# Second feed-forward matrix of an encoder block: Strassen's seven products for eight in three quarters of it, weight sums added in place by DMAs

## The chip, the core and the metric

The kernel runs on one core of a Trainium2 chip. The core has five engines, each with its own instruction queue that is worked through in order: PE (TensorE, matrix products into PSUM, eight banks of 128 x 512 float32), ACT (ScalarE), DVE (VectorE), POOL (GpSimd) and SP (SyncE). They meet only through semaphores. Sixteen DMA engines move data between HBM and SBUF; transfers are issued from the queues of SP, ACT and POOL. The metric is the device time of one execution in microseconds.

## The reference

One encoder block in float32 on 256 tokens of width 2048. What matters here is its last part, the feed-forward part:

```python
h = _layernorm(DEEPNORM_ALPHA * h + mix, ln1_g[l], ln1_b[l])
ff = jnp.square(jax.nn.relu(h @ w_ff1[l])) @ w_ff2[l]
h = _layernorm(DEEPNORM_ALPHA * h + ff, ln2_g[l], ln2_b[l])
```

`w_ff1` is 2048 x 8192, `w_ff2` is 8192 x 2048. Before it stand a gated linear attention branch, a Hyena branch (short convolution, long convolutions by transforms), their gates and an output projection, none of which the change touches in what it computes.

## The kernel before

**Precision.** Every float32 matrix product is made of three products of a narrower format: a value is split into a high part (a cast, on ACT) and a low part (value less high part, on DVE), in `split_hi_lo` (L84 to L86), and hi x hi, hi x lo and lo x hi are summed in PSUM. Weights come from HBM unsplit, so every weight passes through ACT and DVE once.

**Weights.** All weights lie in `wblk`, an array of blocks of 128 x 2048, in the order in which they are used. `fetch` (L95) takes the next block: a DMA on SP into one of three `raw` buffers, then two splits of 128 x 1024 into the `whi` and `wlo` buffers (three each). `next_block` fetches one more and gives the oldest. `resident` loads the last blocks of a stage into their own tiles.

**First feed-forward matrix.** `ff1(qi)` makes one quarter (2048 columns) of the hidden activations, channels on the partitions: for each of 16 blocks of 128 channels `channel_products` runs 16 products of 128 x 512 (both parts of the activation at once, L146) and 16 of 128 x 256 (L150). `channel_sum` adds the two halves of the PSUM bank (ACT L158, DVE L159). Each pair of blocks is squared behind a relu (DVE L1078) and split into the tile `f` that the second matrix reads.

**Second feed-forward matrix.** `ff2(qi)` adds one quarter's share to the residual: four groups of 512 output columns, each with four weight blocks. `token_products` goes through a block's four pieces of 128 x 512 (128 hidden channels by 512 output columns), and for both blocks of 128 tokens runs three products (L205 to L207): 24 products of 128 x 512 a weight block. `add_ff` adds the PSUM sum to `z1`, the residual (L1092 in the first quarter, where it also scales the residual, L1094 later).

**Order.** The quarters run as `ff1(0), ff1(1), ff2(0), ff1(2), ff2(1), ff1(3), ff2(2), ff2(3)`. The scheduler of the framework orders each engine's queue by program order, priorities and a timeline of its own. The last column group of the last quarter uses weights that were made resident, and the final layer norm is worked into it.

**PSUM and SBUF.** Four PSUM banks are `mm` (`psum_main`) and four `sd` (`psum_side`). The tile `zr` has four rows of 2048: two are `z1`, two hold the scale and shift rows of a layer norm.

**Adding DMAs.** The short convolution (`short_conv`) has DMAs that add: `nc.gpsimd.dma_start(dst, src, accum_op=ALU.add)` on L742 adds SBUF rows shifted by one partition to a tile in SBUF. Its large ones have 127 partitions of 4 KB.

Of the kernel before, what the change touches and what calls it, by code (L numbers as in the profile page):

```python
# [9 lines left out]
F32 = mybir.dt.float32  # L10
F32R = mybir.dt.float32r
# [16 lines left out]
CW = D // NCH  # L28
QT = 4
W_OUT_END = 177  # L30
OPENING = 5
PIECES = tuple((k, 1) for k in range(6)) + tuple((k, 2) for k in range(6, KT, 2))

# [9 lines left out]
def block_kernel(  # L43
# [40 lines left out]
    def split_hi_lo(hi, lo, src):  # L84
        return (nc.scalar.copy(hi, src),  # L85
                nc.vector.tensor_tensor(lo, src, hi.bitcast(F32), op=ALU.subtract))  # L86
# [44 lines left out]
    def next_block():  # L131
        fetch()
        return queue.popleft()
# [3 lines left out]
    def channel_psum(name):  # L137
        return psum_main(name).rearrange("p (a b) -> p a b", a=2)
# [19 lines left out]
            nc.scalar.activation(low, ps[:, 1], AF.Copy, scale=scale)  # L158
            nc.vector.scalar_tensor_tensor(dst, ps[:, 0], scale, low, op0=ALU.mult, op1=ALU.add)  # L159

    def channel_pair(act, name, dst=None, scale=1.0, begun=None):
        if dst is None:
            dst = base.tile([P, 2, L], F32, tag="sum", name=f"{name}_s")
        for c in range(2):
            if begun:
                ps, parts, n = begun.pop(0)
                finish_block(ps, act, parts, n)
            else:
                ps = channel_psum(f"{name}_{c}")
                parts = next_block()  # L170
                for h in range(2):
                    channel_products(ps, act, parts[h], range(8 * h, 8 * h + 8))
            channel_sum(dst[:, c], ps, f"{name}_l{c}", scale)
            pump()
        return dst

    def high_by_tokens(ps, act, half, kts, ts):
        for kt in kts:
# [55 lines left out]
    def act_tile(pool, tag, name):  # L234
        return pool.tile([P, KT, 2, L], F32R, tag=tag, name=name)
# [679 lines left out]

    tc.keep_in_program_order(nc.scalar.preload_act_table_set("natural_log_exp_and_others"))

    def resident(slots):
        parts = []
        for hi, lo in slots:  # L920
# [4 lines left out]
            for h in range(2):  # L925
                cs = slice(h * 1024, (h + 1) * 1024)
                split_hi_lo(hi[:, cs], lo[:, cs], raw[:, cs])
            parts.append([(hi[:, 0:1024], lo[:, 0:1024]), (hi[:, 1024:], lo[:, 1024:])])
        return parts

    def halves(pool, tag, name):
        t = pool.tile([P, 4, D], F32R, tag=tag, name=name)
# [39 lines left out]
    rows1 = load_rows(0)  # L972
    turn_b, turn_i = dfth, dftl
    for i, t in ((0, turn_b), (1, turn_i)):
        raw = ep.tile([P, 4, P], F32, tag="aff", bufs=1, name=f"turn{i}")
# [19 lines left out]
    stop_at[0] = nblk  # L995
    hT = act_tile(ep, "hT", "hT")
    lows = []
    for tb in range(NT):
# [34 lines left out]
            turn(at, n)  # L1033


    fts = {}

    def begin_three():
        blocks = [queue.popleft(), [], []]
        hx, lx = (ep.tile([P, D], F32R, tag=t, name=f"{t}_f") for t in ("xh", "xl"))  # L1040
# [29 lines left out]
        fetch()  # L1070
        return begun

    def ff1(qi):
        begun = begin_three() if qi == 0 else []
        f = act_tile(ep, "f", f"f{qi}") if qi % 2 == 0 else act_tile(base, "xT", f"f{qi}")
        for c2 in range(8):
            r = channel_pair(hT, f"f{qi}_{c2}", begun=begun)
            sq = nc.vector.scalar_tensor_tensor(r, r, 0.0, r, op0=ALU.max, op1=ALU.mult)  # L1078
            s = slice(2 * c2, 2 * c2 + 2)
            split_hi_lo(f[:, s, 0], f[:, s, 1], r)  # L1080
            if qi == 0 and 2 <= c2 < 6:
# [3 lines left out]
        fts[qi] = f  # L1085

    st2 = ep.tile([P, NT, 8, 6], F32, tag="bst", bufs=2, name="bst2")

    def add_ff(ps, tb, at, n, qi, last=False):
        zc = z1[:, tb, at:at + n]  # L1090
        if qi == 0:
            nc.vector.scalar_tensor_tensor(zc, zc, ALPHA, ps, op0=ALU.mult, op1=ALU.add)  # L1092
        else:
            nc.vector.tensor_tensor(zc, zc, ps, op=ALU.add)  # L1094
        if qi == QT - 1:
            for i in range(n // 256):
                nc.vector.bn_stats(st2[:, tb, at // 256 + i, :], zc[:, i * 256:(i + 1) * 256])
            if not last:
                nc.vector.tensor_tensor(zc, zc, rows2[:, 0, at:at + n], op=ALU.mult)

    def ff2(qi, groups=4):
        for g in range(groups):
            pss = token_group(fts[qi], f"w2_{qi}{g}")
            for tb in range(NT):
                add_ff(pss[tb], tb, g * 512, 512, qi)

    ff1(0)
    rows2 = load_rows(2)
    ff1(1)
    ff2(0)  # L1110
    ff1(2)
    ff2(1)
    ff1(3)
    ff2(2)
    stop_at[0] = nblk - 4
    ff2(3, 3)
    parts = resident(halves(ep, "f", "wr2") + halves(ep, "hT", "wr3"))
    minus = ep.tile([P, P], F32, tag="minus", name="minus")
    nc.vector.tensor_scalar(minus, ident, -1.0, None, op0=ALU.mult)
    unit = ep.tile([P, P], F32R, tag="unit", name="unit")  # L1120
    nc.scalar.copy(unit, ident)
    zg = tuple(ep.tile([P, D], F32R, tag=t, name=f"{t}_z") for t in ("xh", "xl"))
    for at in (0, 768):
        split_hi_lo(zg[0][:, at:at + 768], zg[1][:, at:at + 768], z1[:, 1, at:at + 768])

    def affine(tb, at, n, rs, nb):
        zc = z1[:, tb, at:at + n]
        t = ep.tile([P, 512], F32, tag="aff", bufs=1, name=f"aff{tb}_{at}")[:, 0:n]
# [7 lines left out]
    token_products([ps], fts[3], parts, [0], 0)  # L1136
    pss = [psum_main(f"w2_33_1{ch}") for ch in range(2)]
    add_ff(ps, 0, 1536, 512, 3)
# [4 lines left out]
    column_products([None, pss], fts[3], parts, [1], 0)  # L1143
    CENTRED = ((0, 512), (512, 512), (1024, 256), (1280, 256))
    po = {}
    for at, n in CENTRED[:3]:
        po[at] = psum_side(f"lo{at}")
        for part in zg:
            tc.keep_in_program_order(MM(po[at], unit, part[:, at:at + 512], start=(part is zg[0]), stop=False))
    po[1280] = po[1024][:, 256:]  # L1150
    add_ff(pss[0][:, 0:256], 1, 1536, 256, 3, last=True)
    late = z1[:, 1, 1536:2048]
    with tc.high_priority(), tc.issue_after(done.ins):
        add_ff(pss[1][:, 0:256], 1, 1792, 256, 3, last=True)
# [12 lines left out]
        nc.vector.tensor_tensor(rs, y, t, op=ALU.mult)  # L1167
# [8 lines left out]
def _layout(a):  # L1176
# [24 lines left out]
    for i in range(NCH // 2):  # L1201
# [1 line left out]
    f1 = chan(a["w_ff1"][0])  # L1203
    w2 = a["w_ff2"][0]
    f1q = [f1[16 * i:16 * (i + 1)] for i in range(QT)]
    f2q = [tok(w2[D * i:D * (i + 1)]) for i in range(QT)]
    g1, g2 = tok(seg["g"][:, :D]), tok(seg["g"][:, D:])
    wblk = np.concatenate(
        [chan(ga), chan(seg["q"]), chan(seg["k"]), tok(seg["r"]), tok(seg["v"]), g1]
        + ubl + [g2, tok(a["w_hy_o"][0]), tok(a["w_out"][0])]  # L1210
        + [f1q[0], f1q[1], f2q[0], f1q[2], f2q[1], f1q[3], f2q[2], f2q[3]], axis=0)
# [100 lines left out]
```

## Time and profile before

| | |
|---|---|
| median of three runs | 1826.89 us (1826.2 to 1827.17) |
| profiled execution, its own time and its span | 1826.2 us |
| matrix products on TensorE | 8931 |
| weight blocks loaded (`raw<-wblk`, 1024 KB each) | 300 |
| median time from issue to landing of such a load | 4.9 us |

Engines in the profile are PE, PEld (weight loads of TensorE, which run beside its products), DVE, ACT, POOL and SP. In the DMA rows q1 is the queue that SP issues to, q0 the one of POOL and q10 the one of ACT. A row of a group of instructions gives line, engine, operation, tiles, shapes and count, then the busy time and the mean duration in ns, then the idle time of the engine ahead of them and who ended it. A row of waits gives who waited for whom, the sum, the number and the longest. In a stretch of the trace the columns are the busy time (and count) of PE, PEld, DVE, ACT and POOL, the granted clock, the DMA share and GB/s. A row of the POOL line gives shortest, median and longest duration in ns.

### The profile page before, as it was taken

Reading aid. Unit: us, or ns where it says so; the run is one execution under the profiler, and the core shown is the slowest. Engines: PE = TensorE matmul, PEld = TensorE weight load, DVE = VectorE, ACT = ScalarE, POOL = GpSimd, SP = SyncE. Lnnn points to the kernel's source line nnn. Section 1 sums busy time; section 2 is a strip of 40 time slices with the busy share of each in tenths; the row PEclk is TensorE's granted clock in tenths of the full one; section 3 lists DMA queues with packets and bytes.
Section 4 is the critical chain, followed back from the end, with each engine's and each line's share of the span. In section 5 each row is a group of like instructions: output and inputs, shape, how many; then the busy total and the mean of one; then the engine's idle time right before and its main releaser. Section 6 shows DMA issues by size and latency. Waiting matters only on the chain.

```text
span 1826.2 us, 22887 instructions
## 1 busy us (share of the span) xinstructions
PE 1817.0 (99%) x8931; PEld 1533.8 (84%) x8931; DVE 1286.8 (70%) x1587; ACT 924.1 (51%) x1207; POOL 80.4 (4%) x121
## 2 busy tenths in 40 slices
PE   9999999999999999999999999999999999999998
PEld 7888888888888888888888889888888888888887
DVE  6789887875689899898755567666545655565467
ACT  6678668865444444444544445444434443443332
POOL 1011110000111101020000000000000000000000
PEclk9999999999999999999999999999999999999999
DMA  8668765345788979796544763545554555555453
GB/s 326 222 257 293 253 220 204 141 162 210 235 281 255 320 249 274 259 281 230 215 186 185 288 252 137 210 185 188 193 196 186 193 195 187 195 195 187 188 197 123
DMA packets 65452, 399.55 MB, mean 219 GB/s; under 512 B 8280, under 2 KB 10856, under 8 KB 24640
## 3 DMA queue, kind: packets, MB, share of 16 engines
q1 hardware_dynamic: 47808, 336.61, 49.1%
q0 software_dynamic: 10480, 41.81, 9.9%
q10 hardware_dynamic: 7056, 19.67, 3.0%
q8 instruction: 70, 1.15, 0.2%
q14 instruction: 38, 0.31, 0.0%
HBM read 369.28 MB, written 16.25 MB: 211 GB/s over the span
## 4 chain that ended last, share of the span: by engine, by line
PE 97%; DMA 1%; DVE 1%; ACT 0%; issue 0%; SPq 0%; DVEq 0%; POOL 0%; ACTq 0%
PE f L146 12%; PE f L150 6%; PE w L205 6%; PE w L207 6%; PE w L206 6%; PE g L206 3%; PE g L205 3%; PE g L207 3%; PE ux L207 3%; PE ux L206 3%; PE ux L205 3%; PE k L146 2%; PE v L206 2%; PE v L205 2%; PE v L207 2%; PE go L206 2%
## 5 line engine op out<-in xcount | busy, mean ns | idle before, releaser
L86 DVE TENSOR_TENSOR wlo<-raw,whi 128x1024 fp32r<-128x1024 f32 x584 | 712.3, 1222 | 356.5 <-ACT whi L85 353.4
L85 ACT CAST whi<-raw 128x1024 fp32r<-128x1024 f32 x584 | 614.0, 1053 | 576.1 <-PE w L207 186.5
L146 PE MATMUL f<-hT,whi 128*128 128x512 f32 x984 | 235.1, 391 | 0.0
L146 PEld LDWEIGHTS f<-hT,whi 128*128 128x128 f32 x984 | 180.8, 188 | 35.0
L206 PE MATMUL w<-wlo,f 128*128 128x512 f32 x480 | 186.7, 389 | 0.0
L207 PE MATMUL w<-whi,f 128*128 128x512 f32 x480 | 186.7, 389 | 0.0
L205 PE MATMUL w<-whi,f 128*128 128x512 f32 x480 | 167.4, 389 | 0.0
L150 PEld LDWEIGHTS f<-hT,wlo 128*128 128x128 f32 x984 | 126.2, 191 | 4.8
L150 PE MATMUL f<-hT,wlo 128*128 128x256 f32 x984 | 127.7, 283 | 0.0
L158 ACT ACTIVATE f_l<-f 128x256 f32<-128x256 f32 x64 | 24.6, 384 | 162.2 <-PE f L146 159.3
L207 PEld LDWEIGHTS w<-whi,f 128*128 128x128 f32 x480 | 90.1, 188 | 18.8
L205 PEld LDWEIGHTS w<-whi,f 128*128 128x128 f32 x480 | 90.1, 188 | 18.7
L206 PEld LDWEIGHTS w<-wlo,f 128*128 128x128 f32 x480 | 90.1, 188 | 18.7
L159 DVE SCALAR_TENSOR_TENSOR f_s<-f,f_l 128x256 f32<-128x256 f32 x64 | 27.2, 425 | 105.0 <-ACT f_l L158 105.0
L206 PE MATMUL g<-wlo,xT 128*128 128x512 f32 x256 | 100.1, 391 | 0.0
L207 PE MATMUL ux<-whi,xT 128*128 128x512 f32 x256 | 99.9, 390 | 0.0
L207 PE MATMUL g<-whi,xT 128*128 128x512 f32 x256 | 99.8, 390 | 0.0
L206 PE MATMUL ux<-wlo,xT 128*128 128x512 f32 x256 | 99.6, 389 | 0.0
L205 PE MATMUL g<-whi,xT 128*128 128x512 f32 x256 | 93.8, 392 | 0.0
L205 PE MATMUL ux<-whi,xT 128*128 128x512 f32 x256 | 89.7, 389 | 0.0
L206 PEld LDWEIGHTS g<-wlo,xT 128*128 128x128 f32 x256 | 48.1, 188 | 10.1 <-DVE wlo L86 0.2
L206 PEld LDWEIGHTS ux<-wlo,xT 128*128 128x128 f32 x256 | 48.1, 188 | 10.1
(428 smaller groups left out, 3235.4 us busy)
## 6 DMA issues: line engine op xcount, KB each, us to landing
raw<-wblk SPq DMA_DIRECT2D x300, 1024.0 KB, 4.9
Td<-T POOLq DMA_DIRECT2D x32, 384.0 KB, 5.5
conv_sb<-conv_rows SPq DMA_DIRECT2D x12, 1024.0 KB, 11.7
Tl<-Td POOLq DMA_DIRECT2D x16, 768.0 KB, 9.1
w<-w4s ACTq DMA_DIRECT2D x16, 512.0 KB, 5.7
xw<-first SPq DMA_DIRECT2D x5, 896.0 KB, 13.4
zr<-ln_rows ACTq DMA_DIRECT2D x4, 1024.0 KB, 10.5
cx<-shift POOLq DMA_DIRECT2D x8, 508.0 KB, 8.4
```

Of the source, the lines that this page charges most:

```text
L85: return (nc.scalar.copy(hi, src), nc.vector.tensor_tensor(lo, src, hi.bitcast(F32), op=ALU.subtract))
L86: nc.vector.tensor_tensor(lo, src, hi.bitcast(F32), op=ALU.subtract))
L146: MM(ps[:, :, ts], hi[:, js], act[:, kt, :, ts], start=(kt == 0 and opens), stop=(kt == KT - 1))
L150: MM(ps[:, 0, ts], lo[:, js], act[:, kt, 0, ts], start=False, stop=False)
L158: nc.scalar.activation(low, ps[:, 1], AF.Copy, scale=scale)
L159: nc.vector.scalar_tensor_tensor(dst, ps[:, 0], scale, low, op0=ALU.mult, op1=ALU.add)
L205: MM(pss[tb], sh, wh, start=(kt == 0), stop=False)
L206: MM(pss[tb], sh, wl, start=False, stop=False)
L207: MM(pss[tb], sl, wh, start=False, stop=(kt == KT - 1))
```

## The change

For three of the four quarters the second matrix is taken in blocks of 2 x 2: 256 hidden channels by 1024 output columns by 256 tokens, each halved in every direction. Eight block products become seven, by Winograd's form of Strassen's scheme. Four forms of the activations are sums and differences (`forms`: three subtractions on DVE), the other three are blocks themselves. The weight side needs sums of pieces of 128 x 512, and these are made by DMAs that add into the loaded tile.

One weight load (`ring_load`) holds 1536 of the four pieces' 2048 columns. There are 48 of them, called slots here, 8 for each of two column groups of each quarter. For slot `p`, in a ring of four tiles:

- `plain_split(p)` splits the three pieces as loaded (1536 columns). Then a DMA on POOL adds the fourth piece from HBM to two of the three (512 KB).
- `pair_split(p)` splits these two sums (1024 columns), and two DMAs on POOL follow: a piece from HBM is added to the first of them (256 KB), and that sum is added, from SBUF to SBUF, to the third (256 KB).
- `last_split(p)` splits these two (1024 columns). With that the seven weight forms have been made.

The products of a slot come in three parts: `plain` in slot `p`, the pair one slot later, the last two sums two slots later. Between them each slot runs one block of the first matrix for the next quarter, whose weights come in half blocks (`half_load`, `half_split`) through three buffers of their own. The seven sums of a column group stay in PSUM over eight slots, so seven banks are taken and one is left for the first matrix. `take_sum` brings them into `z1` and into `zacc`, which takes the two rows that held the layer norm's scale and shift, and `join_sums` puts them together at the end (16 operations of 512 columns). The last quarter keeps its eight products. The block order in `wblk` alternates between the matrices.

```diff
-    ff2(0)
-    ff1(2)
-    ff2(1)
-    ff1(3)
-    ff2(2)
-    stop_at[0] = nblk - 4
-    ff2(3, 3)
...
+    def plain_split(p):
+        raw, n = ring_tile(p), FF_PAIRS + 2 * p
+        hi = ep.tile([P, D], F32R, tag="xh", name=f"b_h{p}")[:, 0:1536]
+        lo = ep.tile([P, 1536], F32R, tag="wx", name=f"b_l{p}")
+        split_hi_lo(hi, lo, raw[:, 0:1536])
+        nc.gpsimd.dma_start(raw[:, 0:1024].rearrange("p (a b) -> p a b", a=2),
+                            wblk[n, :, None, 1536:2048].broadcast_to([P, 2, 512]), accum_op=ALU.add)
+        pieces_of[p, 0] = list(zip(units(hi), units(lo)))
+
+    def pair_split(p):
+        raw, n = ring_tile(p), FF_PAIRS + 2 * p
+        hi, lo = weight_half(n, 0)
+        split_hi_lo(hi, lo, raw[:, 0:1024])
+        nc.gpsimd.dma_start(raw[:, 0:512], wblk[n, :, 512:1024], accum_op=ALU.add)
+        nc.gpsimd.dma_start(raw[:, 1024:1536], raw[:, 0:512], accum_op=ALU.add)
+        pieces_of[p, 1] = list(zip(units(hi), units(lo)))
+
+    def last_split(p):
+        raw = ring_tile(p)[:, 0:1536].rearrange("p (u c) -> p u c", c=512)[:, 0:3:2]
+        fa_slot(4)
+        hi, lo = (t[:, 7168:8192] for t in fa)
+        split_hi_lo(*(t.rearrange("p (u c) -> p u c", c=512) for t in (hi, lo)), raw)
+        pieces_of[p, 2] = list(zip(units(hi), units(lo)))
...
+    def forms(i, plain=False):
+        q, slot = quads(i), fa_slot(i)
+        if plain:
+            split_hi_lo(slot[:, 0, 0:4], slot[:, 1, 0:4], q)
+            return
+        split_hi_lo(slot[:, 0, 0:3], slot[:, 1, 0:3], q[:, 1:4])
+        t = base.tile([P, 4, P], F32, tag="dftl", name=f"fw{i}")
+        TT = nc.vector.tensor_tensor
+        TT(t[:, 0:2], q[:, 0:1].broadcast_to([P, 2, P]), q[:, 1:3][:, ::-1], op=ALU.subtract)
+        TT(t[:, 2], q[:, 1], t[:, 0], op=ALU.subtract)
+        TT(t[:, 3], q[:, 3], t[:, 2], op=ALU.subtract)
+        split_hi_lo(slot[:, 0, 3:7], slot[:, 1, 3:7], t)
...
+    def form_products(pss, p, which, ks):
+        i = p % 8
+        slot = fa_slot(i)
+        for k, (wh, wl) in zip(ks, pieces_of.pop((p, which))):
+            ps, f = pss[k], FORM[k]
+            sh, sl = slot[:, 0, f], slot[:, 1, f]
+            MM(ps, sh, wh, start=(i == 0), stop=False)
+            MM(ps, sh, wl, start=False, stop=False)
+            MM(ps, sl, wh, start=False, stop=(i == 7))
+        if i == 7:
+            for k in ks:
+                take_sum(p // 16, p // 8 % 2, k, pss[k])
...
+    def half_split(j):
+        hi, lo = weight_half(FF_PAIRS + 1 + j // 2 * 2, j % 2)
+        split_hi_lo(hi, lo, half_at.pop(j))
+        half_parts[j] = (hi, lo)
+        if j + 3 < 2 * SLOTS:
+            half_at[j + 3] = half_load(j + 3)
...
+                at = 2 * c2 + c
+                if at == 12:
+                    for j in range(3):
+                        half_at[j] = half_load(j)
+            sq = squares(c2)
+            forms(c2)
+            if c2 == 5:
+                for j in range(3):
+                    half_at[j] = half_load(j)
...
+    def ff_pairs():
+        pss = [psum_side(f"w{j}") if j < 4 else psum_main(f"w{j}") for j in range(7)]
+        joins = []
+        for s in range(SLOTS + 2):
+            if s < SLOTS:
+                form_products(pss, s, 0, (0, 1, 2))
+                if s + 1 < SLOTS:
+                    plain_split(s + 1)
+            if 1 <= s <= SLOTS:
+                form_products(pss, s - 1, 1, (3, 4))
+            if s < SLOTS:
+                pair_split(s)
+            if 2 <= s:
+                form_products(pss, s - 2, 2, (5, 6))
+                if s == SLOTS - 7:
+                    joins = join_sums(0)
+            if s + 2 < SLOTS:
+                ring_load(s + 2)
+            if s >= 10 and (s - 10) % 16 < 8:
+                forms((s - 10) % 16, s >= 2 * 16 + 10)
+            if s < SLOTS:
+                ps = channel_psum(f"f{s // 16 + 1}_{s % 16}")
+                for h in range(2):
+                    channel_products(ps, hT, half_parts.pop(2 * s + h), range(8 * h, 8 * h + 8))
+                    if h == 0 and 1 <= s:
+                        last_split(s - 1)
+                    if s + 1 < SLOTS:
+                        half_split(2 * s + 2 + h)
+                i, c = divmod(s % 16, 2)
+                quad_sum(i, c, ps, f"f{s // 16 + 1}_l{s % 16}")
+                if c:
+                    squares(i)
```

The relu and the square of the hidden activations, one operation on DVE before, are two passes on ACT now (`squares`). Scratch tiles at the end of the kernel (`own`, `spare`, `zg`) are laid into other buffers.

More of the change, by code (lines that the diff above doesn't have):

```diff
@@ L916, in block_kernel, with resident_pieces @@
     tc.keep_in_program_order(nc.scalar.preload_act_table_set("natural_log_exp_and_others"))
-    def resident(slots):
-        parts = []
-        for hi, lo in slots:
+    def resident_pieces(parts):
+        for part in parts:
             n = fetched[0]
@@ L924, in resident @@
             nc.sync.dma_start(raw, wblk[n])
[L925 to L928, printed above, removed]
-        return parts
+            for h, (hi, lo) in enumerate(part):
+                split_hi_lo(hi, lo, raw[:, h * 1024:(h + 1) * 1024])
+        return parts
+    def resident(slots):
+        return resident_pieces([[(hi[:, c:c + 1024], lo[:, c:c + 1024]) for c in (0, 1024)] for hi, lo in slots])
     def halves(pool, tag, name):
@@ new lines, in block_kernel, with quads @@
+    first_quads = {}
+    def quads(i):
+        m = i % 5 if ring else 1 + i % 2
+        if m not in first_quads:
+            if m == 1:
+                first_quads[m] = base.tile([P, 4, P], F32, tag="dfth", name="fr1")
+            elif m == 2:
+                first_quads[m] = base.tile([P, 4, P], F32, tag="sum", name="fr2")
+            else:
+                spare = ring_tile((0, None, None, 1, 2)[m])[:, 1536:2048]
+                first_quads[m] = spare.rearrange("p (a b) -> p a b", b=P)
+        return first_quads[m]
@@ new lines, in block_kernel, with __getitem__, ring_load, units @@
+    class Quarter:
+        def __getitem__(self, at):
+            _, kt, part, ts = at
+            return fa_slot(kt // 2)[:, part, ((1, 0), (3, 2))[kt % 2][ts.start // P]]
+    SLOTS = 48
+    def ring_load(p):
+        nc.sync.dma_start(ring_tile(p)[:, 0:1536], wblk[FF_PAIRS + 2 * p, :, 0:1536])
+    pieces_of = {}
+    def units(t):
+        return [t[:, k * 512:(k + 1) * 512] for k in range(t.shape[1] // 512)]
+    def plain_split(p):
[6 more added lines that the diff above has]
+        pieces_of[p, 0] = list(zip(units(hi), units(lo)))
@@ L1087, in block_kernel, with add_ff @@
     st2 = ep.tile([P, NT, 8, 6], F32, tag="bst", bufs=2, name="bst2")
-    def add_ff(ps, tb, at, n, qi, last=False):
+    def add_ff(ps, tb, at, n, last=False):
         zc = z1[:, tb, at:at + n]
[L1091 to L1099, printed above, removed]
@@ new lines, in add_ff, with quarters @@
+        if not last:
+            nc.vector.tensor_tensor(zc, zc, rows2[:, 0, at:at + n], op=ALU.mult)
+    ff1_first()
+    for p in range(2):
+        ring_load(p)
+    plain_split(0)
+    for j in range(2):
+        half_split(j)
+    ff_pairs()
+    rows2 = load_rows(2)
+    f3 = Quarter()
+    for n in range(3):
+        fetch()
+    for g in range(3):
+        pss = token_group(f3, f"w2_3{g}")
+        for tb in range(NT):
+            add_ff(pss[tb], tb, g * 512, 512)
+    def quarters(*tiles):
+        at = [t[:, k:k + 1024] for t in tiles for k in range(0, t.shape[1], 1024)]
+        return [[(at[0], at[1]), (at[2], at[3])], [(at[4], at[5]), (at[6], at[7])]]
```

171 lines of the change are left out of this document (125 added, 46 removed).

## The prediction

> **What bounds the kernel now.** I read the page's first sections and its chain of waits, then the waits of the feed-forward part alone (1040 us to the end), then stretches of that part.
>
> ```profile
> span 1826.2 us, 22887 instructions
> ...
> PE 1817.0 (99%) x8931; PEld 1533.8 (84%) x8931; DVE 1286.8 (70%) x1587; ACT 924.1 (51%) x1207; POOL 80.4 (4%) x121
> ...
> PEclk9999999999999999999999999999999999999999
> DMA  8668765345788979796544763545554555555453
> ...
> PE 97%; DMA 1%; DVE 1%; ACT 0%; issue 0%; SPq 0%; DVEq 0%; POOL 0%; ACTq 0%
> ```
>
> TensorE is the bound: 99% busy, 97% of the chain, at full granted clock throughout. Every matmul taken away is worth its time, as long as nothing else becomes the bound. In the last sixteen slices DMA is half busy and POOL does nothing.
>
> ```profile
> DVE wlo L86 <- ACT whi L85: 188.6, 187, 1.9
> ACT whi L85 <- PE w L207: 186.5, 115, 1.7
> ACT f_l L158 <- PE f L146: 159.3, 62, 2.7
> ...
> ACT whi L85 <- DMA raw<-wblk: 3.9, 2, 3.2
> ```
>
> Here ScalarE and VectorE wait for TensorE (to give a weight buffer back), hardly ever for a transfer: 3.9 us in all. So there is spare time on every engine but TensorE.
>
> **What the change removes.** The first row below is a stretch that is second-matrix products alone, the others are the sums that close one first-matrix block each.
>
> ```profile
> 1310.00:1376.00 66.00, 66.00 (x293) 54.66 (x292) 33.71 (x32) 25.32 (x24) 0.00 (x0) 1.00 0.51 192
> ```
> ```profile
> 1454.49 0.42 DVE L159 SCALAR_TENSOR_TENSOR f_s<-f,f_l 128x256 f32<-128x256 f32 x1 [1.85 <-ACT f_l L158]
> ...
> 1460.12 0.42 DVE L159 SCALAR_TENSOR_TENSOR f_s<-f,f_l 128x256 f32<-128x256 f32 x1 [1.60 <-ACT f_l L158]
> ...
> 1465.62 0.42 DVE L159 SCALAR_TENSOR_TENSOR f_s<-f,f_l 128x256 f32<-128x256 f32 x1 [1.86 <-ACT f_l L158]
> ```
>
> A 512-wide product costs 66.00/293 = 0.2253 us; a first-matrix block (1465.62-1454.49)/2 = 5.57 us. Old weight block plus first-matrix block: 24 x 0.2253 + 5.57 = 10.98 us. A new slot has 21 products: 4.73 + 5.57 = 10.30 us. The built order has 144 matmuls fewer and no other added on TensorE, so the removal is 144 x 0.2253 = **-32.4 us**, spread over 48 slots.
>
> **What it adds to VectorE and ScalarE.** Durations by shape, feed-forward part:
>
> ```profile
> L86 DVE TENSOR_TENSOR wlo<-raw,whi 128x1024 fp32r<-128x1024 f32 x262 | 320.3, 1224 | 190.5 <-ACT whi L85 188.6 <-PE f L184 1.8
> L85 ACT CAST whi<-raw 128x1024 fp32r<-128x1024 f32 x262 | 274.9, 1050 | 228.2 <-PE w L207 186.5 <-PE wo L207 21.2 <-PE f L146 14.9
> ...
> L159 DVE SCALAR_TENSOR_TENSOR f_s<-f,f_l 128x256 f32<-128x256 f32 x64 | 27.2, 425 | 105.0 <-ACT f_l L158 105.0
> L158 ACT ACTIVATE f_l<-f 128x256 f32<-128x256 f32 x64 | 24.6, 384 | 162.2 <-PE f L146 159.3 <-PE f L184 2.9
> ...
> L86 DVE TENSOR_TENSOR f<-f_s,f 128x512 fp32r<-128x512 f32 x32 | 21.9, 685 | 0.7 <-ACT f L85 0.7
> L85 ACT CAST f<-f_s 128x512 fp32r<-128x512 f32 x32 | 19.9, 622 | 9.9 <-DVE f_s L1078 9.9
> L1094 DVE TENSOR_TENSOR zr<-zr,w 128x512 f32<-128x512 f32 x23 | 14.8, 681 | 1.0 <-PE w L207 1.0
> ```
>
> A slot splits 1536 + 1024 + 1024 + 2 x 1024 columns. By the step from 512 to 1024 columns (0.54 us) the 1536-wide subtraction is 1.22 + 0.54 = 1.76 us, so VectorE has 1.76 + 4 x 1.22 + 0.43 = 7.07 us a slot. In 16 slots the activations' forms come on top: three subtractions of 256, 128 and 128 columns (some 0.42 + 0.28 + 0.28 = 0.98 us by the same slope) and low parts of 384 and 512 (1.24); taking sums adds 7 x 0.68 in 8 slots. The fullest are at some 9.9 of 10.30 us, so VectorE fits, though barely. ScalarE: 1.48 + 4 x 1.05 + 0.38, two squaring passes every second slot (0.62 a slot), forms 1.1: at most 7.8. Both work beside TensorE, priced at nothing; without that cover they'd cost what exceeds 10.30. One PSUM bank is left for first-matrix blocks; emptying it (0.38 + 0.43) lies beside the 4.73 us of products that come before its next use. The eight joining operations a column group, 0.68 each, lie beside later products.
>
> **DMA time.** Loads fall from 2048 to 1792 KB a slot (1.835 MB); the adding DMAs write 1024 KB (1.049 MB). Adding DMAs aren't new here: the short convolution, L742, has them, so their price is in the trace. First loads alone in the feed-forward part (1200 to 1700 us), then 480 to 492 us, where the engines are saturated, then 517 to 519 us, where an add runs alone.
>
> ```profile
> q1 hardware_dynamic: 13089, 95.30, 50.9%
> ```
> ```profile
> q1 hardware_dynamic: 517, 3.77, 80.4%
> q0 software_dynamic: 180, 0.52, 22.2%
> ...
> cv<-conv_sb POOLq DMA_DIRECT2D x1, 508.0 KB, 10.9
> ```
> ```profile
> q0 software_dynamic: 48, 0.20, 96.2%
> ```
>
> Columns: packets, MB, share of 16 engines. Loads take 500 x 0.509/95.30 = 2.67 us a MB. An add takes 12 x 0.222/0.52 = 5.12 us a MB among loads, twice the 12 x 0.804/3.77 = 2.56 of loads there, and 2 x 0.962/0.20 = 9.6 alone. A slot needs 1.835 x 2.67 = 4.90, plus 1.049 x 5.12 = 5.37 (or 10.07 at the lone price): 10.27 us, or 14.97. I take the first, since loads are nearly always queued here; even so the engines go from half busy to as full as TensorE.
>
> **The chain of adds.** The third add of a slot (on POOL) waits for the second to land; the last split waits for the third. Landings, whole run, then one add issued into idle DMA engines (470 to 480 us):
>
> ```profile
> cx<-conv_sb POOLq DMA_DIRECT2D x8, 508.0 KB, 8.9
> ...
> yr<-yd POOLq DMA_DIRECT2D x6, 256.0 KB, 4.3
> ```
> ```profile
> q0 software_dynamic: 172, 0.52, 49.9%
> ...
> cv<-conv_sb POOLq DMA_DIRECT2D x1, 508.0 KB, 8.9
> ```
> ```profile
> L742 POOL DMA_DIRECT2D cx<-conv_sb x16: 756/856/1152, 514.6 to 796.2; - x16
> ```
>
> A 256 KB add is not in the trace. It lands no sooner than the plain 256 KB copy, 4.3 us. Alone, the 508 KB add less half its data time is 8.9 - 10 x 0.499/2 = 6.4; among saturated engines 10.9 - 12 x 0.222/2 = 9.6. I take 7.0, nearest the lone row, since loads come in pieces of 512 and 768 KB.
>
> In the built order VectorE does, after the last split of one slot, two half splits with the block's sum between, the 1536-wide split, then the pair split that lets the next slot's second add go. In-order engines so close a loop over two slots: cast 1.05, subtractions 1.22 + 1.22 + 0.43 + 1.22 + 1.76 + 1.22, two landings: 8.1 + 14.0 = 22.1 us, 11.05 a slot, over TensorE's 10.30. In the 16 form slots 0.98 joins the loop: 11.54. What is late next is the split of half a first-matrix block, queued behind the last split, and TensorE waits for it. The cost is 32 x 0.75 + 16 x 1.24 = **+43.8 us**; at 4.3 us a landing it is 0 (the loop is 8.35), at 9.6 it is 48 x 3.35 + 8 = +169.
>
> The other loop on POOL, the 512 KB add (8.9) held behind the third add: 8.9 + pair split 2.27 + 7.0 + issue 0.86 = 19.0 over two slots, 9.5, decides nothing. POOL issues three adds a slot, 2.6 us of 10.3.
>
> The Trainium skill ("DMA: Bandwidth & Descriptors", section "Anatomy of one DMA") fits a GpSimd-issued DMA as about 2.0 us plus bytes over 436 GB/s, an estimate of 2.6 us for 256 KB. By it the loop would be (8.1 + 5.2)/2 = 6.7 us and the sum -32.4 + 6 = -26. The trace disagrees: by that rule the 508 KB add would land in 3.2 us, and the row has 8.9.
>
> **Edges.** At the start the adds trail two slots; at the end two landings and the last split (16.3 us) lie behind one block (5.57), twelve products (2.7) and pieces of the fourth quarter. Between 0 and 6 us each; I take 3 + 3 = **+6**. Three half-block loads are issued twice in the first quarter: 1.6 MB, 4.2 us of half-idle DMA, the second held on SP until the first lands, with weight loads behind it. Three loaded blocks (16.7 us) hide it; without them up to 4.8 us. Two loads of ring and half buffers move far ahead on SP, where they could hold weight loads likewise.
>
> **Sum:** 1826.2 - 32.4 + 43.8 + 6 = 1843.6 us. The profiled execution is itself the 1826.2 run; the median of the runs is 0.7 above: **1844 us**.
>
> **Rivals.**
> - *The adds land in time* (the other side, faster). If a 256 KB add lands within 5.6 us, the loop is under 10.30 even in the form slots ((8.1 + 0.98 + 11.2)/2 = 10.14) and TensorE stays the bound: 1826.9 - 32.4 + 6 = 1800. The sign turns where the mean loop equals the old slot less the edges, (8.1 + 0.33 + 2L)/2 = 10.98 - 6/48, so L = 6.6, just over the lone landing. For it: ring and lag leave more than a slot for each landing; against: DMA at 10.27 of 10.30 has no idle time to land adds early. The skill's rule would be this case.
> - *Saturated landings*: 9.6 us each, the loop 13.65, 1826.9 - 32.4 + 169 + 6 = 1970. For it the 10.9 row; against, a longer slot empties the DMA queue, so it should settle below.
> - *Adds at the lone price* throughout: 14.97 us a slot, DMA the bound, 1827 + 48 x 3.99 + 6 = 2025. For it the 9.6; against, queued loads brought it to 5.12.
>
> **Chances.** Forecast's case, 1831 to 1900 us: 0.42. In time, under 1823: 0.38, and 0.06 for its meeting with the forecast around no change. Saturated: 0.09. Lone price: 0.05. A measurement tells about 0.2%, 3.7 us, from no change: faster 0.38, same 0.06, slower 0.56. The range, 1798 to 1920, takes in the faster case and leaves out most of the last two; the likeliest case's own is 1831 to 1900.
>
> **What would show it.** Right: 8787 matmuls; DMA in the feed-forward slices at nines; q0 at 41.8 + 50.3 = 92 MB; block sums some 11.1 us apart, wider in the form slots; ScalarE waiting for adding DMAs at the last split, and TensorE for ScalarE or VectorE behind it. Wrong: sums 10.3 apart with TensorE unbroken (first rival), a POOL wait for the second add near 9 us (second), q0 far over 5 us a MB with full engines (third).

## The result, and the profile after

The changed kernel takes 1913.56 us (median of four runs, 1910.49 to 1915.39), the kernel before 1826.69 us beside it: a ratio of 1.0474, 95% interval 1.0459 to 1.0488. It is 87 us slower. The forecast was 1844, 17 us slower: the direction is right, the time lies inside the forecast's wide range (1798 to 1920), but outside the likeliest case's own (1831 to 1900), and the loss is five times the forecast one.

First the page of the changed kernel: span, busy time, the slices of TensorE, of its clock and of DMA, the queues, and the chain that ended last.

```profile
span 1913.6 us, 23461 instructions
...
PE 1835.4 (96%) x8787; PEld 1514.7 (79%) x8787; DVE 1380.1 (72%) x1725; ACT 1028.3 (54%) x1351; POOL 222.8 (12%) x265
...
PE   9999999999999999999999999888989888898898
...
PEclk9999999999999999999999999899999999999999
DMA  8678875455979797975548645689999999999853
...
q0 software_dynamic: 37360, 92.16, 24.8%
...
issue 20%; POOL 6%; PE 5%; DMA 3%; DVE 1%; ACT 0%; POOLq 0%; ACTq 0%; DVEq 0%
POOL ring L1153 2%; POOL ring L1161 2%; DMA ring<-ring 2%; POOL ring L1162 1%; DMA ring<-wblk 1%; PE w L199 1%; PE w L201 1%; PE w L200 1%; DVE wlo L87 0%; PE w L963 0%; PE w L962 0%; PE w L961 0%; PE f L147 0%; ACT fa L86 0%; PE lo L1393 0%
```

The 144 products are gone (8787 of 8931). The page follows the chain of waits back only to 1242 us: its shares sum to 35% of the span, so they can't be set beside the 97% that TensorE had of the whole span before. In that part the adds stand where TensorE stood: their instructions on POOL (L1153, L1161 and L1162 are the first, second and third add of a slot), their transfers, and "issue", of which 291 of 379 us lie directly behind the second add's issue, while that transfer is under way. TensorE's 5% is nearly all the last quarter's products. DMA is at nines where it was at fives. TensorE still looks 96% busy on the page, but only because the change touches a third of the span; in the stretch from 1400 us on it is 89%:

```profile
1400.00:1500.00 100.00, 89.43 (x426) 69.66 (x425) 61.42 (x68) 53.75 (x66) 23.70 (x24) 1.00 0.97 231
```

Who waits there, in the part where the slots have settled (1273 to 1797 us), and how long the transfers take from issue to landing (whole run):

```profile
POOL ring L1162 <- DMA ring<-wblk: 300.0, 42, 9.8
ACT fa L86 <- DMA ring<-ring: 215.1, 41, 8.1
DVE fa L87 <- ACT fa L86: 163.3, 42, 7.1
...
PEld w L1230 <- DVE fa L87: 36.3, 37, 1.1
...
DVE b_l L87 <- ACT b_h L86: 25.5, 20, 1.6
```
```profile
ring<-wblk POOLq DMA_DIRECT2D x48, 512.0 KB, 7.6
...
ring<-wblk POOLq DMA_DIRECT2D x48, 256.0 KB, 7.8
ring<-ring POOLq DMA_DIRECT2D x48, 256.0 KB, 7.3
```

This is the chain of the forecast, link by link: POOL holds the third add until the second has landed, ScalarE holds the last split until the third has, VectorE waits for ScalarE, TensorE for both. Once round the loop, POOL first, then ScalarE (start, duration, instruction, idle time before it and its releaser):

```profile
1404.58 0.98 POOL L1161 DMA_DIRECT2D ring<-wblk  x1
1412.66 0.85 POOL L1162 DMA_DIRECT2D ring<-ring  x1 [7.09 <-DMA ring<-wblk]
...
1429.07 0.92 POOL L1161 DMA_DIRECT2D ring<-wblk  x1
```
```profile
1420.23 1.05 ACT L86 CAST fa<-ring 128x1024 fp32r<-128x1024 f32 x1 [3.21 <-DMA ring<-ring]
```

Second add issued at 1404.58, third at 1412.66 (8.08 later), last split at 1420.23 (7.57), and 8.84 of splits behind it until the second add two slots on. That is 24.49 us for two slots. (Over 40 settled slots the three parts are 8.28, 7.39 and 9.44 us in the mean.) The sums that close the first-matrix blocks give the mean:

```profile
L1112 DVE TENSOR_TENSOR fr<-f,f_l x25: 413/416/423, 1200.0 to 1812.6; 128x256 f32<-128x256 f32 x25
```
```profile
L1112 DVE TENSOR_TENSOR ring<-f,f_l x22: 414/417/419, 1297.4 to 1762.6; 128x256 f32<-128x256 f32 x22
L1112 DVE TENSOR_TENSOR fr<-f,f_l x21: 413/416/417, 1273.1 to 1796.0; 128x256 f32<-128x256 f32 x21
```

All 48 slots (first row, which has every second sum: from the last block of the first quarter to the last block of all) take 612.6 us, where 48 x 10.98 = 527.0 before: +85.6, nearly all of the 87. The other two rows are 43 sums from 1273.1 to 1796.0: a settled slot takes 522.9/42 = 12.45 us. The five before them take 73.0 us, the last 16.7.

### The profile page after: what moved, and what is told of

Its sections match the earlier page's. It is cut to its first block, busy times and chain, and to the rows that moved or that the text cites. A ratio compares the mean times of both kernels' runs of the same rounds, so it can differ in the third digit from the quotient of the medians.

```text
span 1913.6 us, 23461 instructions
## 1 busy us (share of the span) xinstructions
PE 1835.4 (96%) x8787; PEld 1514.7 (79%) x8787; DVE 1380.1 (72%) x1725; ACT 1028.3 (54%) x1351; POOL 222.8 (12%) x265
## 3 DMA queue, kind: packets, MB, share of 16 engines
q0 software_dynamic: 37360, 92.16, 24.8%
## 5 line engine op out<-in xcount | busy, mean ns | idle before, releaser
L86 ACT CAST whi<-raw 128x1024 fp32r<-128x1024 f32 x392 | 412.7, 1054 | 406.7 <-PE ux L201 87.5
L87 DVE TENSOR_TENSOR wlo<-raw,whi 128x1024 fp32r<-128x1024 f32 x392 | 477.1, 1221 | 205.7 <-ACT whi L86 204.3
L147 PEld LDWEIGHTS f<-hT,whi 128*128 128x128 f32 x984 | 183.9, 194 | 59.7 <-DVE fr L1112 13.3
L87 DVE TENSOR_TENSOR fa<-ring,fa 128x1024 fp32r<-128x1024 f32 (+2 forms) x60 | 65.9, 1098 | 177.6 <-ACT fa L86 177.6
L86 ACT CAST fa<-ring 128x1024 fp32r<-128x1024 f32 (+2 forms) x60 | 56.8, 947 | 235.7 <-DMA ring<-ring 229.2
L87 DVE TENSOR_TENSOR wlo<-fraw,whi 128x1024 fp32r<-128x1024 f32 x96 | 116.7, 1216 | 1.1 <-ACT whi L86 1.1
L87 DVE TENSOR_TENSOR b_l<-ring,b_h 128x1536 fp32r<-128x1536 f32 x48 | 84.2, 1754 | 29.5 <-ACT b_h L86 29.4
L1153 POOL DMA_DIRECT2D ring<-wblk x48 | 59.6, 1242 | 388.7 <-DVE b_l L87 388.2
L86 ACT CAST whi<-fraw 128x1024 fp32r<-128x1024 f32 x96 | 100.4, 1046 | 0.0
L87 DVE TENSOR_TENSOR wlo<-ring,whi 128x1024 fp32r<-128x1024 f32 x48 | 58.4, 1218 | 29.8 <-ACT whi L86 29.8
L1162 POOL DMA_DIRECT2D ring<-ring x48 | 40.9, 852 | 328.9 <-DMA ring<-wblk 328.9
L86 ACT CAST b_h<-ring 128x1536 fp32r<-128x1536 f32 x48 | 70.5, 1469 | 3.1 <-PE w L1231 3.1
```

The costliest lines, as they stand in the source:

```text
L86: return (nc.scalar.copy(hi, src), nc.vector.tensor_tensor(lo, src, hi.bitcast(F32), op=ALU.subtract))
L147: MM(ps[:, :, ts], hi[:, js], act[:, kt, :, ts], start=(kt == 0 and opens), stop=(kt == KT - 1))
L1153: nc.gpsimd.dma_start(raw[:, 0:1024].rearrange("p (a b) -> p a b", a=2), wblk[n, :, None, 1536:2048].broadcast_to([P, 2, 512]), accum_op=A ...
L1162: nc.gpsimd.dma_start(raw[:, 1024:1536], raw[:, 0:512], accum_op=ALU.add)
```

## Is it the chain of two landings?

**One link taken out.** The third add reads its piece from HBM, so nothing has to land before it is issued. Its bytes stay, its values are others (one of the seven sums).

```diff
-        nc.gpsimd.dma_start(raw[:, 1024:1536], raw[:, 0:512], accum_op=ALU.add)
+        nc.gpsimd.dma_start(raw[:, 1024:1536], wblk[n, :, 512:1024], accum_op=ALU.add)
```

> The third add of a slot takes its source from HBM instead of the sum that the second add makes, so it no longer waits for the second (the third sum gets other values). Same bytes, same count of adds, same last split. Theory (in-order loop through two landings in a row): one landing leaves the loop, 8.1 + 1.0 + 7.8 = 16.9 us over two slots, so a slot falls from 12.45 to what TensorE or the DMA engines allow, 10.3 to 11.1, and the start's 16.5 us slots go too: 1805 to 1845 us. Rival (the DMA engines, 94 to 99% busy, set the slot by their bytes): the bytes are the same, so the time stays at 1900 to 1920.

Measured: 1825.13 us, ratio 0.9992 (0.9983 to 1.0001). The same bytes and the same number of adds, 88 us less: so it is the order in which they must land, not what they move. The profile shows what is left when the chain is gone:

```profile
1400.00:1500.00 100.00, 99.49 (x502) 83.17 (x501) 72.45 (x75) 62.26 (x72) 26.99 (x27) 1.00 1.04 270
```
```profile
ring<-wblk POOLq DMA_DIRECT2D x48, 512.0 KB, 7.3
ring<-wblk POOLq DMA_DIRECT2D x96, 256.0 KB, 9.9
```

DMA is fuller than in the changed kernel (1.04 against 0.97) and a 256 KB add lands later (9.9 us, second and third adds together), yet TensorE is back to 99% here, and to 96 to 98% in the other stretches from 1300 to 1700 us. A settled slot is 10.70 us, not 10.30, by the block sums as above, and the first five still take 62.0 us, where the theory had the slow start gone. Whether those 0.4 us are bandwidth or the one landing that is left wasn't taken apart.

**One link more.** The third add is cut into two of 128 KB, the second reading what the first wrote. Same bytes; half of the third sum has other values.

```diff
-        nc.gpsimd.dma_start(raw[:, 1024:1536], raw[:, 0:512], accum_op=ALU.add)
+        nc.gpsimd.dma_start(raw[:, 1024:1280], raw[:, 0:256], accum_op=ALU.add)
+        nc.gpsimd.dma_start(raw[:, 1280:1536], raw[:, 1024:1280], accum_op=ALU.add)
```

> The third add is cut in two of 128 KB, and the second of these takes its source from what the first wrote, so one more landing stands in the chain (half of the third sum gets other values). Same bytes. Theory: the two-slot loop grows by about one landing of 5 to 6 us, less 1.2 us for a half split that the built order now puts ahead of the last split: 12.45 + 2 = 14.3 to 14.8 a slot, 1990 to 2030 us. Rival (DMA bytes): no change, 1905 to 1925.

Measured: 2002.86 us, ratio 1.0965 (1.0946 to 1.0983). One more landing on the chain costs 89 us, while DMA empties to eights; a settled slot is 14.73 us, within the theory's 14.3 to 14.8. POOL now waits twice a slot:

```profile
POOL ring L1162 <- DMA ring<-wblk: 315.1, 48, 10.9
...
POOL ring L1163 <- DMA ring<-ring: 193.7, 48, 5.6
```

**No adds at all.** All three are left out (four of the seven sums lack the pieces that they add), everything else stays.

> All three adding DMAs are left out (the products take the weights as loaded, so four of the seven sums are wrong); all loads, splits and products stay. Every theory: TensorE alone sets the slot, 10.30 us: 1797 to 1812 us. If it stays above 1830, VectorE and ScalarE have part of the cost.

Measured: 1794.1 us, ratio 0.9823 (0.9804 to 0.9843); TensorE 1784.1 of 1792.3 us busy in the profiled one of two executions. This is what the seven products are worth: 1826.43 (the kernel before on the same chip) - 1794.1 = 32.3 us, beside a forecast removal of 32.4.

**Is it the adding?** The three DMAs copy and don't add (the sums are not made); order, bytes and waits stay.

```diff
-        nc.gpsimd.dma_start(raw[:, 1024:1536], raw[:, 0:512], accum_op=ALU.add)
+        nc.gpsimd.dma_start(raw[:, 1024:1536], raw[:, 0:512])
```

(and the same for the other two)

> The three adding DMAs of a slot become plain copies of the same bytes, in the same order and with the same waits; the sums they should make are left out (four of the seven sums are other values). Theory (the two landings are long because DMAs that add among full queues take twice a load's time): DMA engines fall from nines to some seven tenths (1.835 MB at 2.67 plus 1.049 MB at 2.67 is 7.7 us of a slot), a 256 KB copy lands in 4.3 to 5.5 us as the plain rows do, the loop is 24.5 - 15.1 + 2 x 5 = 19.4 over two slots, 9.7, under TensorE's 10.30, and the time is 1798 to 1822. Rival (a landing is what any DMA issued from GpSimd takes on this path, adding or not): landings stay at 7 or more, block sums stay near 12 us apart, and the time is 1880 to 1915.

Measured: 1853.79 us, ratio 1.0153 (1.0136 to 1.0171): between the two theories, a miss for both. Queues and landings:

```profile
q0 software_dynamic: 25072, 92.16, 21.1%
```
```profile
ring<-wblk POOLq DMA_DIRECT2D x48, 256.0 KB, 6.8
ring<-ring POOLq DMA_DIRECT2D x48, 256.0 KB, 5.4
```

The two landings fall from 15.1 to 12.2 us, so the loop from 24.9 to 22.0 if nothing else changes, 11.0 a slot; the block sums say 11.57. So adding is worth 59.8 of the 119.5 us that lie between the changed kernel and the one without adds, and the other 59.7 stay with copies in the same chain: two plain copies that wait for each other are too slow as well. (DMA is emptier here too, 0.84 against 0.97 between 1400 and 1500 us; what of the shorter landings is due to that and what to the copy itself wasn't taken apart.)

## Which queue holds the wait?

**The third add on VectorE, where the scheduler puts it.** An addition of two tiles takes the place of the DMA, in the text right behind the pair split.

```diff
-        nc.gpsimd.dma_start(raw[:, 1024:1536], raw[:, 0:512], accum_op=ALU.add)
+        nc.vector.tensor_tensor(raw[:, 1024:1536], raw[:, 1024:1536], raw[:, 0:512], op=ALU.add)
```

> The third add is done by VectorE (one operation of 512 columns, about 0.68 us, behind the second add's landing) instead of a DMA from SBUF to SBUF; same result. Theory: the loop is 8.1 + 1.0 + 0.7 + 7.8 = 17.6 us over two slots, not binding; VectorE at 8 to 10.6 of 10.3 us; slots of 10.3 to 10.7: 1800 to 1820 us, below the kernel before. Rival (DMA bytes): adds fall from 1024 to 768 KB a slot, at 5.8 us a MB 1.5 us a slot less, 12.45 to 10.9: 1835 to 1845.

Measured: 2011.42 us, ratio 1.1005 (1.0988 to 1.1021): a miss for both theories and the slowest kernel of all, though one DMA fewer is on the path. POOL, then VectorE:

```profile
1408.03 0.99 POOL L1161 DMA_DIRECT2D ring<-wblk  x1
1422.36 1.19 POOL L1153 DMA_DIRECT2D ring<-wblk  x1 [13.34 <-DVE b_l L87]
1423.40 1.08 POOL L1161 DMA_DIRECT2D ring<-wblk  x1
```
```profile
1416.74 0.69 DVE L1162 TENSOR_TENSOR ring<-ring 128x512 f32<-128x512 f32 x1 [5.13 <-DMA ring<-wblk]
...
1420.22 1.75 DVE L87 TENSOR_TENSOR b_l<-ring,b_h 128x1536 fp32r<-128x1536 f32 x1
1421.89 1.22 DVE L87 TENSOR_TENSOR wlo<-ring,whi 128x1024 fp32r<-128x1024 f32 x1
```

VectorE itself now waits for the landing, in the slot in which the add was issued, and the next slot's splits, which release the next second add, stand behind it: issue at 1408.03, landing, 0.69 us of addition, splits, issue at 1423.40. One landing in a loop over one slot makes a slot of 15.4 us; two in a loop over two slots made one of 12.45. What counts is landings per slot of slack, together with the work that stands behind each.

**The third add on GpSimd's arithmetic**, in the place of the third DMA, ahead of the last split.

> The third add is one operation of GpSimd on SBUF (128 x 512), in the place that the third DMA had in its queue; same result. Theory: the landing of 7.3 us is replaced by an operation of 1 to 2 us: 8.1 + 1.0 + 7.8 + 1.5 = 18.4 us over two slots; the loop through GpSimd's own queue, 7.8 + 1.5 + 1.2 + 7.6 + 2.3 = 20.4, is 10.2 a slot. Slots of 10.3 to 11: 1805 to 1840 us. If GpSimd's reads and VectorE's second inputs get in each other's way, some more.

Measured: 1875.19 us, ratio 1.0272 (1.0255 to 1.0289), a miss.

```profile
1406.72 1.29 POOL L1166 TENSOR_TENSOR ring<-ring 128x512 f32<-128x512 f32 x1 [8.04 <-DMA ring<-wblk]
1407.96 1.20 POOL L1153 DMA_DIRECT2D ring<-wblk  x1
1408.69 1.39 POOL L1161 DMA_DIRECT2D ring<-wblk  x1
1418.14 1.70 POOL L1166 TENSOR_TENSOR ring<-ring 128x512 f32<-128x512 f32 x1 [8.06 <-DMA ring<-wblk]
```

The operation isn't the trouble (1.29 us). POOL works through its queue in order and waits for the landing of the second add; only then can it issue the next second add: 11.42 us from one addition to the next, 11.78 in the mean. I had moved the arithmetic and left the wait on the queue that issues the adds.

**The last split behind both half splits**, so that TensorE's next block no longer waits for it (ScalarE's and VectorE's halves queued behind those of the second half split).

> The last split is queued behind both half splits and the block's sum on ScalarE and VectorE instead of ahead of them; no DMA changes. Theory: the path from the last split to the next pair split loses 2.9 us of VectorE, so the two-slot loop falls from 24.7 to 21.8, 10.9 a slot, if TensorE does not then wait for the later last split (up to 1.2 us a slot more): 1840 to 1885 us. Rival (DMA bytes): 1905 to 1920.

Measured: 1933.59 us, ratio 1.0579 (1.0554 to 1.0604), a miss.

```profile
1403.44 0.85 POOL L1162 DMA_DIRECT2D ring<-ring  x1 [8.27 <-DMA ring<-wblk]
1403.98 1.53 POOL L1153 DMA_DIRECT2D ring<-wblk  x1
1404.69 1.74 POOL L1161 DMA_DIRECT2D ring<-wblk  x1
1420.13 0.85 POOL L1162 DMA_DIRECT2D ring<-ring  x1 [13.70 <-DMA ring<-wblk]
```
```profile
ring<-wblk POOLq DMA_DIRECT2D x48, 512.0 KB, 10.0
ring<-wblk POOLq DMA_DIRECT2D x48, 256.0 KB, 11.4
```

Another loop binds now, one slot long and in POOL's queue alone. The third add is held until the second has landed; behind it the first add of a later slot and the next slot's second add go out at once, without a wait for a split, and POOL then waits for that landing. Over 40 settled slots the third add starts 11.94 us after the second, and the two issues behind it take 1.2: 13.1 us, and the block sums give a settled slot of 13.29. In the changed kernel the same loop is 8.28 us and issues of some 1.7, an estimated 10 us, and hidden behind the other. Why the adds land so much later than there (7.6 and 7.8) was not settled. What it shows is that taking one loop out is not enough while the third add still waits in POOL's queue.

**The third add on VectorE, queued one slot later**, behind the next slot's pair split. Nothing else changes.

```diff
-        split_hi_lo(hi, lo, raw[:, 0:1024])
+        paired[p] = split_hi_lo(hi, lo, raw[:, 0:1024])
         nc.gpsimd.dma_start(raw[:, 0:512], wblk[n, :, 512:1024], accum_op=ALU.add)
-        nc.gpsimd.dma_start(raw[:, 1024:1536], raw[:, 0:512], accum_op=ALU.add)
...
     def last_split(p):
-        raw = ring_tile(p)[:, 0:1536].rearrange("p (u c) -> p u c", c=512)[:, 0:3:2]
+        full = ring_tile(p)
+        with tc.issue_after(paired[min(p + 1, SLOTS - 1)][1].ins):
+            nc.vector.tensor_tensor(full[:, 1024:1536], full[:, 1024:1536], full[:, 0:512], op=ALU.add)
+        raw = full[:, 0:1536].rearrange("p (u c) -> p u c", c=512)[:, 0:3:2]
```

> The third add is on VectorE again, but queued one slot later, behind the next slot's pair split, so the second add has a whole slot to land before VectorE waits for it; same result. Theory (what counts is which work stands behind a wait for a landing): second add 7.8 + third 0.7 + the 7.1 us of VectorE up to the pair split after next = 15.6 us over two slots, not binding; slots at TensorE's 10.3 to 10.7: 1800 to 1820 us. Rival (the add on VectorE itself costs the time that the same kernel with the add right behind the pair split showed): near 2011. Rival (DMA bytes set the slot, 10.8 with 1024 KB of adds, now 768 KB): 1800 to 1825 too.

Measured: 1803.12 us, ratio 0.9873 (0.9858 to 0.9887): faster than both kernels. The group of the moved additions (1200 to 1790 us), then POOL:

```profile
L1169 DVE TENSOR_TENSOR ring<-ring 128x512 f32<-128x512 f32 x48 | 32.8, 684 | 2.9 <-DMA ring<-wblk 2.9
```
```profile
1406.71 1.19 POOL L1153 DMA_DIRECT2D ring<-wblk  x1 [8.04 <-DVE b_l L87]
1407.75 1.08 POOL L1163 DMA_DIRECT2D ring<-wblk  x1
1417.31 1.19 POOL L1153 DMA_DIRECT2D ring<-wblk  x1 [8.49 <-DVE b_l L87]
```

VectorE waits 2.9 us for these landings in all 48 slots. The second add has a whole slot to land, its 8.6 us (median) fit into 10.3, and POOL waits for a landing only once (1.8 us); otherwise it waits for VectorE's splits, as it should. The same operation on the same engine is 208 us apart by its place in the queue.

## The first slots, and the loads issued twice

**The start, first try.** In the changed kernel's built order the third add of a slot stands ahead of the next slot's first add in slots 0, 2 and 3, so there the landings follow one another. Here it is queued behind it from the start.

```diff
-        nc.gpsimd.dma_start(raw[:, 1024:1536], raw[:, 0:512], accum_op=ALU.add)
+        with tc.issue_after(first_add[min(p + 1, SLOTS - 1)].ins):
+            nc.gpsimd.dma_start(raw[:, 1024:1536], raw[:, 0:512], accum_op=ALU.add)
```

> Only the order of GpSimd's queue at the start changes: the next slot's first add is issued ahead of the third add in every slot (the built order had this from the fifth slot on, and before that the other way round). Theory: in the first four slots all landings of a slot stand in one row, 16.4 us a slot; with the order changed they take 12.5 like the others: 1895 to 1903 us. Rival (the start is slow because TensorE's clock and the buffers have to recover): 1908 to 1918.

Measured: 1902.87 us, ratio 1.0426 (1.0407 to 1.0445), 11 us less than the changed kernel, at the upper end of what the theory gave: the first five slots take 65.2 us where they took 73.0, the settled ones 12.51, as before. The early slots are shorter but not at 12.5, as the theory had them: four of the five take 13.3 to 14.9.

**The start, in the version with the third sum on VectorE.** There the first slots were still 13.2, 15.6 and 13.0 us, since each pair split stood ahead of the next 1536-wide split and so held back its first add. One order more:

```diff
-        paired[p] = split_hi_lo(hi, lo, raw[:, 0:1024])
+        with tc.issue_after(first_of[min(p + 1, SLOTS - 1)][1].ins):
+            paired[p] = split_hi_lo(hi, lo, raw[:, 0:1024])
```

(`first_of[p]` is what the split in `plain_split(p)` returns.)

> The version whose third sum VectorE makes (1803.1 us), with one more order: from the first slot on, a pair split is queued behind the next slot's 1536-wide split. In that version's first slots it stood ahead of it (block sums 13.2, 15.6, 13.0 us apart), so that the next first add was issued only when the one before had landed. Theory (the start is that order): the first slots fall to 10.3 to 11 us and the time to 1793 to 1798. Rival (the first slots are held by transfers into queues still full of the first quarter's loads): block sums there stay at 13 us or more, 1801 to 1805.

Measured: 1794.22 us, ratio 0.9824 (0.9808 to 0.9841), as fast as the kernel without any add. Two stretches and the queue:

```profile
1203.00:1300.00 97.00, 96.85 (x500) 82.77 (x500) 74.66 (x75) 61.58 (x72) 21.14 (x20) 1.00 0.94 243
1300.00:1400.00 100.00, 100.00 (x518) 85.92 (x517) 87.71 (x111) 70.92 (x88) 21.09 (x20) 1.00 0.98 257
```

TensorE is busy without a gap with DMA at 0.98 and VectorE at 88%: a full DMA is no loss as long as nothing waits for a landing that isn't due.

**The half-block loads issued twice**, left out once in the changed kernel and once in the 1803 us version:

```diff
-                at = 2 * c2 + c
-                if at == 12:
-                    for j in range(3):
-                        half_at[j] = half_load(j)
```

> The changed kernel without the second set of the three half-block loads in the first quarter. Prediction's step (hidden): the same as the changed kernel, 1910 to 1917. Rival (the second set holds weight loads back on SP): up to 4.8 us less, 1905 to 1909.

> The version whose third sum VectorE makes behind the next slot's pair split (1803.1), without the second set of the three half-block loads. Hidden: 1802 to 1804.5. Rival (they cost where TensorE is the bound): 1797 to 1801.

Measured: 1914.73 (ratio 1.0482, 1.0467 to 1.0498) and 1804.08 (0.9876, 0.9860 to 0.9893), each 1 us above the kernel with them, with overlapping intervals of the ratio. No cost of theirs shows: they are hidden.

## Why the prediction was right in kind and off in size

- **What bounds before, and the removal (-32.4): right.** Without adds, and with the adds placed well, the kernel gains 32.2 to 32.3 us, and TensorE is full.
- **VectorE and ScalarE beside TensorE: right.** In the fastest version (1794.2 us) VectorE does the forecast's work and 0.68 us more a slot without holding TensorE up; inside the loop of adds the cover failed (below). **The 16 form slots' extra (0.98 in the loop): wrong.** The settled gaps between block sums that hold the first of these subtractions are 12.38 us in the mean, the others 12.49; where the 0.98 us went wasn't taken apart.
- **DMA time: near.** Adds cost 5.12 us a MB in the forecast. Queue 0's share less that of the kernel without adds (row below) is 24.8% of 1913.6 less 10.0% of 1792.3, 295 us for 92.16 - 41.81 = 50.35 MB: 5.87 us a MB. A slot's transfers would then need 4.90 + 1.049 x 5.87 = 11.06 us; yet with the chain cut the same bytes fitted into 10.70, so such a sum of transfer times is no floor. The engines did go to nines. With the chain cut that costs at most 0.4 us a slot; what full engines add to each landing stays open.

```profile
q0 software_dynamic: 10480, 41.81, 10.0%
```

- **The loop of adds (+43.8): the mechanism right, the term mis-sized; this is the step that failed.** Freeing one landing took 88 us away and adding one cost 89. That the two are alike is chance: the first ends at TensorE's 10.30, or near it, the second is about half a landing more in each slot (12.45 to 14.73). But a slot is 12.45 us and not 11.05 to 11.54, so the term is 48 x (12.45 - 10.30) = +103. I took 7.0 us a landing, "nearest the lone row, since loads come in pieces of 512 and 768 KB"; the medians are 7.8 and 7.3, and from issue to the next instruction of the chain it is 8.08 and 7.57. The engines' part is 24.9 - 15.65 = 9.25 us where I had 8.1 (9.08 in form slots). That is 2.5 us a turn in sum, and the loop turns 24 times. Some 1.65 of the 2.5 are the landings. Of the rest 0.6 is a wait that the forecast had at nothing: VectorE waits 25.5 us in 20 of the 42 settled slots (the b_l row above) for ScalarE's cast of the 1536 columns, which in every second slot is queued behind the two squaring passes. The forecast had these passes lie beside TensorE's products; they stand in the loop.
- **Edges (+6): too small.** The first five slots and the last take 73.0 + 16.7 - 6 x 12.45 = 15.0 us over settled ones. I looked at how far the adds trail, not at how the built order starts: there the first slots' landings follow one another. With the loop's 103 and the 32.4 this gives +85.6, what the block sums show. In the run that changes that order the same sum is 65.2 + 15.6 - 6 x 12.51 = 5.7, near the forecast.
- **The other loop on POOL: right here** (7.6 + 2.27 + 7.8 + 0.86 = 18.5 for two slots). What it left out is the loop of one slot in the same queue (a second add's landing and the issues behind it), which binds at 13.1 us when the last split is queued later, and at 11.78 when GpSimd adds.
- **The rivals.** That the adds land in time needed 6.6 us a landing at most for the sign to turn; they were 7.3 and 7.8. It was the right rival to hold high: the landings missed that line by 0.7 and 1.2 us. It came true where the order let it, not where a landing was shorter (8.8 us in the fastest version). Saturated landings (9.6) are not in the changed kernel but were there in others, 9.9 and 11.4. The lone price did not come.
- **The Trainium skill's fit** ("DMA: Bandwidth & Descriptors", "Anatomy of one DMA"), about 2.0 us plus bytes over 436 GB/s, would give an estimated 2.6 us for 256 KB. The trace disagrees with it again: 7.8 and 7.3 us adding, and still 6.8 and 5.4 us for plain copies among these loads.

## What to carry to other kernels

A transfer that must land before the next is issued costs its landing once per turn of the loop that the in-order queues close around it, so count landings against slots of slack, and ask of each wait in whose queue it stands and what stands behind it. Here the same addition on VectorE made a kernel 184 us slower than the one before when it stood behind its own slot's add, and one 23 us faster one slot later. Check the built order of the first few turns as well as the settled one: a line that only keeps it from the start on was worth 9 us.

## What the runs showed of the hardware

An adding DMA is dearer than a copy of the same bytes in three places. It makes more packets (37360 on queue 0 for 92.16 MB, 25072 for copies); it takes 5.87 us of DMA time a MB, where the copies take (21.1% of 1857.8 less 179.2)/50.35 = 4.23; and POOL needs longer to issue it. The issues of the copies, then those of the adds:

```profile
L1153 POOL DMA_DIRECT2D ring<-wblk x48: 714/714/736, 1188.5 to 1743.6; - x48
L1161 POOL DMA_DIRECT2D ring<-wblk x48: 539/567/567, 1201.6 to 1752.9; - x48
```
```profile
L1153 POOL DMA_DIRECT2D ring<-wblk x48: 1182/1196/1532, 1189.3 to 1791.6; - x48
L1161 POOL DMA_DIRECT2D ring<-wblk x48: 870/982/1763, 1202.5 to 1802.4; - x48
```

A landing is not a constant of its size: the 256 KB add from HBM took from 7.7 to 11.4 us (medians) in these kernels (7.8 in the changed one, 8.6 with VectorE's addition one slot later, 9.9 with the chain cut, 11.4 with the last split queued later), and the longest is not in the one with the fullest DMA (1.04 between 1400 and 1500 us where it took 9.9, 0.89 where it took 11.4). GpSimd adds two tiles of 128x512 in 1.29 us (median 1287 ns), VectorE in 0.68.

In the changed kernel's first slots, where TensorE is busy for 81.99 of 97 us, its granted clock is lower as well (third column from the end):

```profile
1203.00:1300.00 97.00, 81.99 (x369) 64.72 (x369) 48.27 (x48) 43.73 (x51) 20.27 (x21) 0.91 0.80 187
```

The fastest version has 1.00 in the same stretch, with TensorE busy for 96.85 us. Gaps alone don't tell the clock: between 1400 and 1500 us the changed kernel has 1.00 at 89.43 of 100 us. What sets it is not shown by these runs.
